# Feed-forward blocks of 768, 768 and 576 tokens instead of 576, 768 and 768, with one product and one addition moved

## The chip, the core and the metric

The kernel runs on one core of a Trainium2 chip. The metric is the device time of one execution in microseconds (us), the median of several runs. The engines are named as in the profile: PE (TensorE, matrix products), PEld (its weight loads), DVE (VectorE), ACT (ScalarE), POOL (GpSimd) and SP (SyncE, which issues most transfers here).

## What is computed

One layer of a streaming encoder over 2048 prompt tokens and 64 sample tokens. The first half (normalisation, the combined input projection, causal convolution, chunk-band attention) is not touched by the change. The second half is, for every token:

```python
merged = sigmoid(g_conv) * conv_out + sigmoid(g_attn) * attn_out
x = x + gt1 * (merged @ w_o)
h2 = rms_norm(x, norm2_g) * (1 + sc2) + sh2
gate, up = split(h2 @ w_ffn_in, 2)            # (1024, 2 * 2816)
x = x + gt2 * ((silu(gate) * up) @ w_ffn_out)  # (2816, 1024)
```

`gt1`, `sc2`, `sh2`, `gt2` come from a conditioning vector of their own for the prompt and for the sample, so the 64 sample tokens need other rows of them.

## The kernel before, in words

**Precision.** Every operand of a product is kept as a high part and a low part (`split`: ACT makes the high part, another engine subtracts it from the source). `mm3` issues three matmuls for each product: high by high, high by low, low by high.

**Blocks.** The second half goes through the tokens in the blocks of `CBLOCKS` (line 36). The sample's 64 tokens are stored ahead of the prompt and lie in the first block, of 576. `token_tiles` cuts a block into tiles of 128 tokens (and one of 64), `tile_chunks` cuts it into two chunks for the merge. For 576 tokens the chunks have 320 and 256 tokens, for 768 they have 384 and 384.

**One block.** For each chunk `merge` multiplies with `w_conv_out` and `w_attn_out` and applies the sigmoid gates, `wo` multiplies with `w_o`, and `residual`, a generator per tile, adds `x`, normalises, transposes and makes the operands `b11 b21 b22 t1 t2 t3 t4` of the next step. Then ten products for the first five gates (`first`, `second`) need `b11` and `b21` alone, which cover the last tiles of `residual`. After them the 22 gates run in pairs (`up`).

**Seven-product scheme, gate and up.** The tokens of a block are taken in two halves and the 1024 inner rows in two halves, so that gate and up column of one `f` are a 2 by 2 by 2 block product with seven products in place of eight: weights `a11 a12 a22` and the sums `s1` to `s4`, each of 128x512. From gate 5 (`EARLY`) on all seven run in this loop, in the order of `up_operands` (line 536): `s2 s3 s1 a12 a22`, `a11` of the next gate, `s4`. Each is 12 matmuls over 288 or 384 columns. Two successive operands make one slab.

**Down product.** In blocks 1 and 2 (`s` true) the pairs of gates 4 to 19 (`PAIRS`) use another seven-product scheme for `w_ffn_out`: `down_pair` with `B11 B21 B22` and the sums `T1` to `T4`, in four groups (`DN`), which `at` places between the products of the next pair at the slabs of `dn_at` (line 544: 0, 1, 3, 4). In block 0 all of it is plain (`down`): eight products' worth for every pair, with no sums. `down` also closes every block with the last gates: it adds the accumulated rows, multiplies by `gt2`, adds the row `x1` (lines 1982 to 1984, all on DVE) and stores the result.

**Weights.** `Weights` loads raw weights, makes the sums on POOL, splits them, and keeps at most five slabs split ahead. The high part is made on ACT, the low part on POOL, or on DVE when the planner's count of POOL's work is more than 4 us ahead of PE's (`BEHIND`, line 456). Sums of gate and up are made once, in block 0, and stored (`sum_d`); in later blocks they are loaded and split again. Weights of kind `fo` and `dn` that are used in more than one block are stored split and then only loaded.

**Order.** `Stream` counts the cost of what has been emitted for each engine; `at(t, f)` runs `f` when PE's count reaches `t`. The order of every engine's queue is thus fixed when the program is built.

Of the kernel before, what the change touches and what calls it, by code (L numbers as in the profile page):

```python
# [35 lines left out]
CBLOCKS = [(0, 576), (576, 1344), (1344, 2112)]  # L36
# [43 lines left out]
def tile_chunks(lo, hi):  # L80

    tiles = token_tiles(lo, hi)
    t, n = tiles[(len(tiles) + 1) // 2 - 1]
    return [(lo, t + n), (t + n, hi)]
# [168 lines left out]
class Weights:  # L253
# [5 lines left out]
    def __init__(self, engines, pool, dram, stream, keys, source, staging, held, kept):  # L259
# [6 lines left out]
        times, raws = {}, {}  # L266
# [119 lines left out]
    def load_on(self, kind):  # L386
        while self.due[kind] and self.free_tag(kind):
            self.load(kind)
# [166 lines left out]
def weight_order():  # L555
# [10 lines left out]
    for s, (lo, hi) in enumerate(CBLOCKS):  # L566
# [13 lines left out]
        yield from (("fo", f) for f in range(NF - 2 if s else NF - 4, NF))  # L580
# [3 lines left out]
def streaming_layer(ctx: ExitStack, tc: tile.TileContext, I, O):  # L584
# [455 lines left out]
    def gate_columns(c0, c1, ct):  # L1040
        g = [half_piece(ct % 2, "tg") for _ in range(2)]
        for j in range(2):
            nc.sync.dma_start(g[j][:, : c1 - c0], g_d[j, ct, :, c0:c1])
        return g

    def load_mixed(c0, c1, i):

        src = [[quarter("cin", i) for _ in range(2)] for _ in range(2)]
        for j, a in enumerate((c_d, o_d)):
            for l in range(2):  # L1050
                nc.sync.dma_start(src[l][j][:, :, : c1 - c0].bitcast(F32), a[l, :, :, c0:c1].rearrange("c p t -> p c t"))
# [546 lines left out]
    def residual(pp, t, n, gt1, a, half, hs, free, last):  # L1598


        which = int(t < SMP)
        x_t = [wk.tile([P, 512], F32, tag="ws", name="x_t", bufs=4) for _ in range(2)]
        for j in range(2):
            nc.sync.dma_start(x_t[j][:n], rows(x_p, x_s, t, n)[:, 512 * j : 512 * j + 512])
# [83 lines left out]
    for s, (lo, hi) in enumerate(CBLOCKS):  # L1688
        tiles = token_tiles(lo, hi)
        half = (hi - lo) // 2  # L1690
        gt1, groups, hs = {}, [], None
        chunks = tile_chunks(lo, hi)
        for i, (c0, c1) in enumerate(chunks):
# [8 lines left out]
            if not groups:  # L1702
                for which in {int(t < SMP) for t, _ in tiles}:
# [39 lines left out]
        hid = [wk.tile([P, 2, 2, CW] if not s else [P, 4, 2, CW // 2], F32R, tag="m0", name="hid"), None]  # L1743
# [40 lines left out]
        def rows_of(f, t, n):  # L1784

            if s:
# [5 lines left out]
        def hidden(f, i, ps):  # L1792
            if s:
# [98 lines left out]
        def up(f, ops, at):  # L1892
# [39 lines left out]
            if f % 2 == 0:  # L1932
# [3 lines left out]
            two = s and f - f % 2 in PAIRS  # L1936
# [15 lines left out]
        def down(fs, ws):  # L1952

            last = fs[-1] == NF - 1
            for i, (t, n) in enumerate(tiles):
# [3 lines left out]
                gt = gt2[int(t < SMP)] if last else None  # L1959
# [12 lines left out]
                for j, ps in enumerate(pss):  # L1972
# [7 lines left out]
                    else:  # L1980
                        if not final:
                            dve.tensor_tensor(ps[:n], ps[:n], dst, ALU.add)
                        dve.tensor_tensor(ps[:n], ps[:n], gt[:n, f], ALU.mult)
                        dve.tensor_tensor(dst, ps[:n], dst if final else x1[j], ALU.add)
                        stream.at(
                            stream.when("dve") + OUT_LAG,
                            lambda t=t, n=n, f=f, dst=dst: nc.sync.dma_start(rows(y_p, y_s, t, n)[:, f], dst),
# [27 lines left out]
        if not s:  # L2015
            W.open("fo", "wfo")
        turns.drain()
# [3 lines left out]
        for f in range(0, NF, 2):  # L2021
            ops = Operands(f)
            if s and f == PAIRS[0]:
                hid[1] = wk.tile([P, 4, 2, CW // 2], F32R, tag="m1", name="hid")
            elif not s and f // 2 % 2 and f >= NF - 4:
                hid[1] = wk.tile([P, 2, 2, CW], F32R, tag="m1", name="hid")

            def at(i, f=f):
                if s and f - 2 in PAIRS:
# [10 lines left out]
        end = NF - 2 if s else NF - 4  # L2040
        ws = [W.get(("fo", f)) for f in range(end, NF)]
        gt2 = {which: gt_row(1, which) for which in {int(t < SMP) for t, _ in tiles}}
# [39 lines left out]
```

## Time and profile before

| | us |
|---|---|
| median of 3 runs | 3047.6 |
| lowest, highest run | 3043.95, 3049.64 |
| profiled execution | 3048.72 |
| its span, first to last instruction | 3046.9 |

The first half of the layer ends at about 1229 us of the span. Block 0 (576 tokens) then runs to about 1785 us, block 1 (768) to about 2409 us and block 2 (768) to the end. Its mean granted TensorE clock is 0.987 of full speed.

In the views below, a row of grouped instructions reads: line, engine, operation, names, form, count, busy time in us, mean ns of one, and the engine's idle time before them with what ended it. A row of a stretch gives its length, then each engine's busy time (with its number of instructions), the granted clock, the busy share of the DMA engines and GB/s. All products come from helpers at one line (L104 is the line of the recorder), so the rows are told apart by tile names: `ps` are the products of gate and up (with `b` or `t` operands) and of the merge (`cin`), `pw` those with `w_o`, `pd` those of the down product; `whi` and `wlo` are the two parts of a weight slab, `wst`, `wup`, `wfo` raw weights, `ws` the weight sums.

### The profile page before, as it was taken

How to read it: one execution, taken by the hardware profiler on the slowest of the kernel's cores; microseconds unless marked ns; L12 is line 12 of the kernel's file. 1: busy time of each engine (PE TensorE's matmuls, PEld its weight loads, DVE VectorE, ACT ScalarE, POOL GpSimd, SP SyncE). 2: the span in 40 equal slices, each digit the busy share in tenths (PEclk: the TensorE clock that was granted, in tenths of full speed). 3: DMA queues.
4: the chain of work that ended last, by engine and by line, in shares of the span. 5: the costliest groups of instructions: out<-in, count | busy, mean ns of one | idle time of the engine just before them, and what ended most of it. 6: DMA issues, size and time to landing. Idle time of an engine off the chain costs nothing. (4 is left out here: it accounts for less than half of the span.)

```text
span 3046.9 us, 44878 instructions
## 1 busy us (share of the span) xinstructions
PE 2936.2 (96%) x16259; PEld 2609.2 (86%) x16259; DVE 2043.0 (67%) x3826; ACT 1254.4 (41%) x2260; POOL 989.7 (32%) x617
## 2 busy tenths in 40 slices
PE   7989898999999999989999999999999999999998
PEld 4789777888878788878998989999999898999997
DVE  4797687877977895467666755655666756366567
ACT  2324432453245257364444424534444244333331
POOL 0200210101011102355677433247767341333331
PEclk9999998999999999999999999999999999999999
DMA  9789788887987788886444686445556965355554
GB/s 336 262 276 309 224 293 267 270 263 265 306 277 247 250 267 274 259 278 218 144 149 142 227 292 202 159 166 190 181 196 202 344 213 189 119 167 174 166 162 174
DMA packets 487084, 693.07 MB, mean 227 GB/s; under 512 B 38485, under 2 KB 316873, under 8 KB 486862
## 3 DMA queue, kind: packets, MB, share of 16 engines
q1 hardware_dynamic: 474581, 672.82, 67.2%
q10 hardware_dynamic: 12280, 17.39, 1.6%
q8 instruction: 128, 2.10, 0.3%
q14 instruction: 95, 0.77, 0.1%
HBM read 505.89 MB, written 184.19 MB: 226 GB/s over the span
## 5 line engine op out<-in xcount | busy, mean ns | idle before, releaser
L104 POOL TENSOR_TENSOR wlo<-wst,whi 128x1024 fp32r<-128x1024 f32 (+1 forms) x180 | 402.6, 2243 | 499.5 <-ACT whi L104 427.6
L104 PE MATMUL ps<-t,whi 128*128 128x384 f32 (+1 forms) x2112 | 505.8, 323 | 10.5 <-DVE t L104 4.8
L104 PE MATMUL pd<-whi,hid 128*128 128x512 f32 (+1 forms) x1400 | 450.3, 391 | 3.4 <-DVE acc L104 3.4
L104 ACT ACTIVATE whi<-wst 128x1024 fp32r<-128x1024 f32 (+1 forms) x269 | 262.0, 978 | 360.5 <-PE ps L104 120.1
L104 PE MATMUL ps<-b,whi 128*128 128x384 f32 (+1 forms) x1584 | 381.1, 326 | 11.4 <-DVE pw L104 4.0
L104 PEld LDWEIGHTS ps<-t,whi 128*128 128x128 f32 x2112 | 370.6, 189 | 18.6 <-ACT u L104 5.5
L104 DVE SCALAR_TENSOR_TENSOR y<-u,wd,y 128x512 f32<-128x512 f32 (+1 forms) x480 | 368.3, 771 | 6.5
L104 PE MATMUL ps<-hh,whi 128*128 128x512 f32 (+2 forms) x992 | 363.6, 367 | 0.0
L104 PE MATMUL ps<-hl,whi 128*128 128x512 f32 (+2 forms) x992 | 346.6, 349 | 0.0
L104 PE MATMUL ps<-hh,wlo 128*128 128x512 f32 (+2 forms) x992 | 346.0, 349 | 0.0
L104 DVE TENSOR_TENSOR acc<-acc,pd 128x512 f32<-128x512 f32 (+1 forms) x440 | 290.5, 684 | 80.4 <-PE pd L104 76.8
L104 PE MATMUL ps<-t,wlo 128*128 128x384 f32 (+1 forms) x1056 | 340.8, 323 | 0.0
L104 PEld LDWEIGHTS pd<-whi,hid 128*128 128x128 f32 (+1 forms) x1400 | 258.1, 184 | 64.7 <-DVE acc L104 6.9
L104 PEld LDWEIGHTS ps<-b,whi 128*128 128x128 f32 x1584 | 278.1, 189 | 14.7 <-DVE pw L104 4.3
L104 PE MATMUL pd<-wlo,hid 128*128 128x512 f32 (+1 forms) x700 | 273.7, 391 | 0.0
L104 PE MATMUL ps<-b,wlo 128*128 128x384 f32 (+1 forms) x792 | 257.1, 325 | 0.0
L104 POOL TENSOR_TENSOR r<-t,mhalf 128x8 f32<-128x8 f32 (+3 forms) x68 | 84.5, 1244 | 390.9 <-DVE t L104 368.0
L104 PEld LDWEIGHTS ps<-hh,wlo 128*128 128x128 f32 x992 | 187.9, 189 | 22.4
L104 POOL TENSOR_TENSOR wlo<-wup,whi 128x1024 fp32r<-128x1024 f32 (+1 forms) x64 | 138.3, 2162 | 208.8 <-ACT whi L104 176.5
L104 PEld LDWEIGHTS ps<-hh,whi 128*128 128x128 f32 x992 | 188.8, 190 | 18.7 <-issue 2.1
L104 PEld LDWEIGHTS ps<-hl,whi 128*128 128x128 f32 x992 | 188.8, 190 | 15.4 <-issue 1.7
L104 PEld LDWEIGHTS ps<-t,wlo 128*128 128x128 f32 x1056 | 199.3, 189 | 0.6
(217 smaller groups left out, 5725.5 us busy)
## 6 DMA issues: line engine op xcount, KB each, us to landing
whi<-w_din_h SPq DMA_DIRECT2D x72, 512.0 KB, 5.9
wlo<-w_din_l SPq DMA_DIRECT2D x72, 512.0 KB, 7.1
wst<-sum_d SPq DMA_DIRECT2D x131, 256.0 KB, 3.0
wmod<-in_w_ada SPq DMA_DIRECT2D x48, 512.0 KB, 8.5
sum_d<-ws SPq DMA_DIRECT2D x88, 256.0 KB, 2.4
wst<-in_w_ffn_in SPq DMA_DIRECT2D x85, 256.0 KB, 3.4
wst<-in_w_ffn_in SPq DMA_DIRECT2D x37, 512.0 KB, 5.4
wst<-in_w_in SPq DMA_DIRECT2D x36, 512.0 KB, 7.1
```

Source lines behind the costliest of these rows:

```text
L104: return f(*args, **kw)
```

## The change

The blocks become (0, 768), (768, 1536) and (1536, 2112). Tokens are renumbered inside the second half: the sample stands at 1536 (`SAT`), at the head of the last block; `stored_at` and `segments` translate to the places where the first half left its results. A range that spans the sample's end needs two transfers. The down product's seven-product scheme is used in blocks 0 and 1 (`SEVEN = 2`), the plain form in block 2. For odd gates from 5 on, `a12` is issued ahead of `s1`; the fourth group of `down_pair` keeps its place behind `s1`, now at slab 5. In the closing `down`, the addition of `x1` goes to GpSimd (`gps`) except in the last two tiles of the last block. Raw `fo` rows of the last block are not loaded before that block's products begin (`limit`), and there only into the two `wfo` buffers.

```diff
-CBLOCKS = [(0, 576), (576, 1344), (1344, 2112)]
+CBLOCKS = [(0, 768), (768, 1536), (1536, 2112)]
+SAT = 1536
+SEVEN = 2
+def block_tiles(lo, hi):
+    head = [(SAT, SMP)] if lo == SAT else []
+    return head + [(u, P) for u in range(lo + SMP * len(head), hi, P)]
+def stored_at(u):
+    return u if u >= SAT + SMP else u - SAT if u >= SAT else u + SMP
+def segments(c0, c1):
+    cuts = [c0] + [c for c in (SAT, SAT + SMP) if c0 < c < c1] + [c1]
+    return [(a - c0, stored_at(a), b - a) for a, b in zip(cuts, cuts[1:])]
...
+            if key[0] == "ca" and n == 2 * SEVEN + 1:
+                self.limit = min(self.limit, len(self.items))
...
-        if kind == "fo" and (self.items[self.due["fo"][0]][0] == "fr" or any(self.items[i][0] == "fi" for i in self.due[""])):
+        if kind == "fo" and (self.limit == 1 << 30 or self.items[self.due["fo"][0]][0] == "fr" or any(self.items[i][0] == "fi" for i in self.due[""])):
             tags = tags[:1]
...
         while self.due[kind] and self.free_tag(kind):
+            if kind == "fo" and self.due[kind][0] >= self.limit:
+                break
...
-    ops = (["s2", "s3", "s1"] if f else ["s3", "s2", "s1"]) + ["a12"] * (f >= EARLY) + ["a22"] + ["a11"] * (EARLY <= f + 1 < NF) + ["s4"]
+    ops = (["s2", "s3"] if f else ["s3", "s2"]) + ["a12"] * (f >= EARLY and f % 2) + ["s1"] + ["a12"] * (f >= EARLY and f % 2 == 0) + ["a22"] + ["a11"] * (EARLY <= f + 1 < NF) + ["s4"]
...
-    return (0, 1, 3, 6 if f == PAIRS[-1] else 4)
+    return (0, 1, 3, 6 if f == PAIRS[-1] else 5)
...
-                if s and f - 2 in PAIRS:
+                if s < SEVEN and f - 2 in PAIRS:
...
         for j in range(2):
-            nc.sync.dma_start(g[j][:, : c1 - c0], g_d[j, ct, :, c0:c1])
+            for o, t, n in segments(c0, c1):
+                nc.sync.dma_start(g[j][:, o : o + n], g_d[j, ct, :, t : t + n])
...
+            def factor():
+                if f >= EARLY:
+                    x = bank("gp")
+                    step(x, "a12", "b21", True, True)
+                    plus(x, x, s1)
+                    silu(c1, x)
+
             if f % 2 == 0:
                 at(0)
+            else:
+                factor()
             step(y, "s1", "t1", False, False)
             plus(v, y, v)
             if f % 2:
-                at(4)
-            if f >= EARLY:
-                x = bank("gp")
-                step(x, "a12", "b21", True, True)
-                plus(x, x, s1)
-                silu(c1, x)
-            if f % 2 == 0:
+                at(5)
+            else:
+                factor()
                 at(1)
...
+                        name = "dve" if hi == T and i >= len(tiles) - 2 else "pool"
                         if not final:
                             dve.tensor_tensor(ps[:n], ps[:n], dst, ALU.add)
-                        dve.tensor_tensor(ps[:n], ps[:n], gt[:n, f], ALU.mult)
-                        dve.tensor_tensor(dst, ps[:n], dst if final else x1[j], ALU.add)
+                        if name == "pool":
+                            dve.tensor_tensor(dst, ps[:n], gt[:n, f], ALU.mult)
+                            stream.after("pool", "dve")
+                            gps.tensor_tensor(dst, dst, x1[j], ALU.add)
+                        else:
+                            dve.tensor_tensor(ps[:n], ps[:n], gt[:n, f], ALU.mult)
+                            dve.tensor_tensor(dst, ps[:n], dst if final else x1[j], ALU.add)
...
         if not s:
             W.open("fo", "wfo")
+        elif not seven:
+            W.limit = 1 << 30
+            W.load_on("fo")
```

Elsewhere `s` is replaced by `seven = s < SEVEN`, `t < SMP` by `t == SAT`, `token_tiles` by `block_tiles`, and the row of `x` or `y` that a tile reads or writes by `stored_at(t)`.

More of the change, by code (lines that the diff above doesn't have):

```diff
@@ L579, in weight_order @@
                     yield from (("fo", f - 2), ("fo", f - 1))
-        yield from (("fo", f) for f in range(NF - 2 if s else NF - 4, NF))
+        yield from (("fo", f) for f in range(NF - 2 if s < SEVEN else NF - 4, NF))
 @with_exitstack
@@ L1688, in streaming_layer @@
     for s, (lo, hi) in enumerate(CBLOCKS):
-        tiles = token_tiles(lo, hi)
+        tiles = block_tiles(lo, hi)
         half = (hi - lo) // 2
+        seven = s < SEVEN
         gt1, groups, hs = {}, [], None
@@ L1702, in streaming_layer @@
             if not groups:
-                for which in {int(t < SMP) for t, _ in tiles}:
+                for which in {int(t == SAT) for t, _ in tiles}:
                     gt1[which] = gt_row(0, which)
@@ L1741, in streaming_layer @@
                 turns.add(gens[i])
-        hid = [wk.tile([P, 2, 2, CW] if not s else [P, 4, 2, CW // 2], F32R, tag="m0", name="hid"), None]
+        hid = [wk.tile([P, 4, 2, CW // 2] if seven else [P, 2, 2, CW], F32R, tag="m0", name="hid"), None]
         early = wk.tile([P, 2 * EARLY - 2, CW // 2], F32, tag="m1", name="early")
@@ L1784, in rows_of @@
         def rows_of(f, t, n):
-            if s:
+            if seven:
                 i, c = divmod(t - lo, half)
@@ L1792, in hidden @@
         def hidden(f, i, ps):
-            if s:
+            if seven:
                 hi, lo = (whole(f, i)[:, j] for j in range(2))
@@ L1935, in up @@
             plus(z, z, u2)
-            two = s and f - f % 2 in PAIRS
+            two = seven and f - f % 2 in PAIRS
             dve.tensor_tensor(z, z, c1, ALU.mult)
@@ L1958, in down @@
                 pss = [ps_g.tile([P, 512], F32, tag="gp", name="pd", bufs=4) for _ in range(2)]
-                gt = gt2[int(t < SMP)] if last else None
+                gt = gt2[int(t == SAT)] if last else None
                 final = last and hi == T and i == len(tiles) - 1
@@ L2039, in streaming_layer @@
         drain()
-        end = NF - 2 if s else NF - 4
+        end = NF - 2 if seven else NF - 4
         ws = [W.get(("fo", f)) for f in range(end, NF)]
-        gt2 = {which: gt_row(1, which) for which in {int(t < SMP) for t, _ in tiles}}
+        gt2 = {which: gt_row(1, which) for which in {int(t == SAT) for t, _ in tiles}}
         x1s = [quarter("x1", 1, F32, (P, 3, 512)) for _ in range(4)]
```

23 lines of the change are left out of this document (13 added, 10 removed).

## The prediction

> **What bounds the kernel now.** I read the page's head first, then stretches of the second half that I cut at the stages of the three blocks.
>
> ```profile
> span 3046.9 us, 44878 instructions
> PE 2936.2 (96%) x16259; PEld 2609.2 (86%) x16259; DVE 2043.0 (67%) x3826; ACT 1254.4 (41%) x2260; POOL 989.7 (32%) x617
> ```
>
> ```profile
> core 0: us, PE busy (x) PEld busy (x) DVE busy (x) ACT busy (x) POOL busy (x), PEclk, DMA share, GB/s
> 1229.00:1340.00 111.00, 106.72 (x622) 94.19 (x623) 59.15 (x118) 51.53 (x83) 44.34 (x21) 0.97 0.82 262
> 1340.00:1425.00 85.00, 72.13 (x443) 66.13 (x443) 56.01 (x99) 47.31 (x91) 48.39 (x36) 0.94 0.77 266
> 1425.00:1720.00 295.00, 291.10 (x1845) 265.17 (x1845) 194.56 (x293) 119.21 (x242) 200.56 (x135) 1.00 0.46 150
> 1785.00:1895.00 110.00, 107.43 (x543) 97.24 (x542) 54.25 (x91) 47.17 (x69) 44.16 (x21) 0.98 0.67 221
> 1895.00:1945.00 50.00, 47.41 (x254) 44.31 (x253) 40.97 (x69) 29.93 (x55) 12.28 (x9) 0.97 0.48 170
> 1945.00:2390.00 445.00, 445.00 (x2341) 417.54 (x2340) 257.17 (x442) 193.04 (x320) 267.74 (x152) 1.00 0.58 192
> 2390.00:2530.00 140.00, 137.79 (x703) 124.38 (x702) 80.17 (x139) 52.49 (x75) 48.00 (x22) 1.00 0.76 256
> 2530.00:2580.00 50.00, 47.37 (x254) 44.45 (x253) 40.53 (x69) 29.92 (x55) 7.04 (x5) 0.97 0.49 172
> 2580.00:3015.00 435.00, 435.00 (x2292) 408.71 (x2291) 249.94 (x431) 157.04 (x258) 153.97 (x65) 1.00 0.50 162
> ```
>
> The first column is the length, the next PE's busy time, so their difference is PE's idle time. In the long stretches of blocks 1 and 2 (1945 to 2390, 2580 to 3015) it is nil: the second half is bound by PE, and there is nothing to win there but matmuls, of which the change removes none. What can move is the idle time at the seams: 4.3 us in block 0's merge (1229 to 1340), 12.9 at its opening (1340 to 1425), 3.9 in its pairs (1425 to 1720), 2.6 in block 1's merge, 2.6 at each of the openings of blocks 1 and 2, and 2.2 where block 1 closes. A wait also costs clock: block 1's opening has a clock of 0.97 over 50 us, that is another 1.5 us behind 2.6 us of idling, block 0's opening 0.94 over 85 us, another 5.1, its merge 0.97 over 111 us, another 3.3. The loss of the openings is thus 18.0, 4.1 and 4.1 us, of block 0's merge 7.6, of block 1's 2.6 + 2.2 (0.98 over 110 us) = 4.8. Then the list of PE's waits in the second half:
>
> ```profile
> PE ps L104 <- DVE t L104: 7.9, 4, 2.4
> PE ps L104 <- DVE pw L104: 4.0, 1, 4.0
> PE ps L104 <- ACT u L104: 3.9, 7, 0.6
> PE ps L104 <- DVE early L104: 3.6, 1, 3.6
> PE pd L104 <- DVE acc L104: 3.4, 6, 0.6
> PE ps L104 <- DVE v L104: 2.8, 2, 1.9
> PE pw L104 <- POOL wlo L104: 2.1, 1, 2.1
> ```
>
> Not one of them is for a weight slab in the pairs: the preparation of weights keeps up everywhere, even in block 0, where it is heaviest.
>
> [...]
>
> **The work is the same.** Two blocks of 768 with seven products and one of 576 with the plain form stand in both kernels, with equal tiles, so the matmuls are equal in number and shape. The sum has only changes of waits.
>
> **1. Openings.** They belong to the block's shape and to what else its engines do. In block 0 the first wait comes from the first splits of the gate weights:
>
> ```profile
> 1348.32 5.01 POOL L104 TENSOR_TENSOR wlo<-wst,whi 128x512 fp32r<-128x512 f32 x4
> 1353.88 1.15 ACT L104 ACTIVATE xn<-x,r 128x1024 f32<-128x1024 f32 x1 [3.81 <-POOL r L104]
> ```
>
> Four low parts hold GpSimd for 5.0 us, the row's inverse root `r` stands behind them, ACT waits 3.8 us, and PE's wait of 3.6 for `early` follows. In the last block these weights come split from memory, so the 576 form there loses this wait, and the waits for `v` (2.8), which I take to stand behind first splits of `fo` on DVE, since `fo` 0 to 3 are only loaded then. What is left is 18.0 - 3.6 - 2.8 - 1.7 (a third of its clock loss) = 9.9. Block 0 in the 768 form: 4.1 as in block 1, plus that ACT wait of 3.8 and 1.7 of clock = 9.6. Block 1: 4.1. Sum 23.6 for 26.2: -2.6. Best, all three like block 1: 12.3, -13.9. Worst, blocks 0 and 2 both like the present block 0: 40.1, +13.9. I stay near the middle, since each half of block 0's loss has a row of its own.
>
> **2. Merges.** The second chunk of 256 tokens waits for gate columns:
>
> ```profile
> 1307.81 0.39 PE L104 MATMUL ps<-cin,whi 128*128 128x256 f32 x1 [2.27 <-DVE t L104]
> ```
>
> Chunks of 384 (blocks 1 and 2) have no such wait. Block 0 gains these 2.3 us and 1.7 of clock; the last block now has the 256 chunk, and twenty more transfers (two for one in the first chunk: sixteen of gates, four of mixed columns) on SP. I give half of it back: -2. Ends -4 and +4.
>
> **3. Handover from block 0 to block 1.** Its 2.1 us wait for `wlo` (4.8 with the clock and what is left of idling) arises where the plain closing with four gates meets the first `w_o` slab; the handover from block 1 to 2, with the form that both will now have, shows only the closing's waits. Half of it: -2.4; ends -4.8 and +3.
>
> **4. Odd gates' `a12`.** It removes and adds nothing, it changes the order.
>
> ```profile
> 1490.74 0.54 PE L104 MATMUL ps<-t,whi 128*128 128x288 f32 x2 [0.56 <-ACT u L104]
> 1527.37 0.53 PE L104 MATMUL ps<-t,whi 128*128 128x288 f32 x2 [0.55 <-ACT u L104]
> ```
>
> Once in a pair (36.6 us) PE waits 0.56 us for ACT's copy of `y` before `s1` accumulates on it; with `a12` between there are twelve more matmuls, well over the wait. All seven waits go: -3.9. In 768 blocks a group of `down_pair` stands there already and no wait shows: 0. Ends -3.9 and 0 (if ACT is late by more).
>
> **5. Closing additions.** Each tile of a 768 block's closing takes DVE three pairs of additions and products:
>
> ```profile
> 3025.68 1.29 DVE L104 TENSOR_TENSOR pd<-pd,acc 128x512 f32<-128x512 f32 x2
> 3028.07 1.27 DVE L104 TENSOR_TENSOR acc<-pd,x 128x512 f32<-128x512 f32 x2
> ```
>
> The third pair is the one that moves; from one tile's start to the end of its third pair are 3.7 us, and PE's 3.4 us for `acc` in six waits (three in each closing) say that it runs out of banks by some 0.6 us a tile. Without the third pair DVE is faster than PE: -3.4. GpSimd gets 12 additions a block, at 1.31 us (below) 15.7 us, in a stretch where it is one third busy (48.0 of 140 us); behind them in its queue stand splits of the next block's merge weights. If those come late like the 2.1 us wait above, with 1.7 of clock, at two handovers: +7.6. Ends -4 and +7.6.
>
> **6. Block 0's pairs.** Here the change adds load: the down sums and splits move from block 1, where they stood alone, to the block that also makes all gate sums.
>
> ```profile
> L104 POOL TENSOR_TENSOR wlo<-wst,whi 128x1024 fp32r<-128x1024 f32 x10 | 24.1, 2411 | 7.0 <-ACT whi L104 7.0
> L104 POOL TENSOR_TENSOR wlo<-ws,whi 128x512 fp32r<-128x512 f32 x8 | 10.3, 1304 | 2.9 <-ACT whi L104 2.9
> L104 POOL TENSOR_TENSOR wlo<-wup,whi 128x1024 fp32r<-128x1024 f32 x4 | 9.6, 2406 | 2.9 <-DMA wfo<-in_w_ffn_out 1.8 <-ACT whi L104 1.2
> L104 POOL TENSOR_TENSOR wlo<-wfo,whi 128x512 fp32r<-128x512 f32 x6 | 7.9, 1315 | 2.9 <-ACT whi L104 2.9
> L104 POOL TENSOR_TENSOR ws<-wfo 128x512 f32<-128x512 f32 x4 | 5.3, 1317 | 10.2 <-DMA wfo<-in_w_ffn_out 10.2
> L104 POOL TENSOR_TENSOR ws<-wfo,ws 128x512 f32<-128x512 f32 x4 | 5.2, 1310 | 0.3
> ...
> L104 DVE TENSOR_TENSOR acc<-acc,pd 128x512 f32<-128x512 f32 x42 | 27.4, 683 | 2.8 <-PE pd L104 2.4
> ```
>
> Two pairs in 88 us (42 additions of `pd`, 21 to a pair): 62.4 us of GpSimd, 31.2 a pair. Block 0's eight gate sums come on top:
>
> ```profile
> L104 POOL TENSOR_TENSOR ws<-wst 128x512 f32<-128x512 f32 x5 | 7.6, 1512 | 3.6 <-DMA wst<-in_w_ffn_in 3.6
> ...
> L104 DVE TENSOR_TENSOR wlo<-ws,whi 128x512 fp32r<-128x512 f32 x10 | 12.4, 1241 | 1.5 <-ACT whi L104 0.9
> L104 DVE TENSOR_TENSOR wlo<-wfo,whi 128x1024 fp32r<-128x1024 f32 x2 | 2.5, 1225 | 1.6 <-ACT whi L104 1.6
> ```
>
> At 1.51 us they take 12.1: 43.3 of 44 us, 98%. But here DVE made at least 14 of the 36 half slabs of two pairs (the 1024 rows count twice). The same share, some 9 of the 21 of a pair, at 1.24 us costs DVE 11 us beside its 25.4 (257.17 of 445 us): 36 of 44, and leaves GpSimd 32. So it fits, as in block 0 now, whose own demand was as near its PE time. What it costs is delay: DVE's 21 additions, 0.683 us each, must follow PE group by group, and a split of 1.24 us among them holds a bank. They fill 14.3 of the 44 us, so 3 of the 9 splits meet them; at half a split each that is 1.9 us a pair, 15 in eight pairs. The nearest row is against it: no wait for `acc` in block 0's pairs at this share. I take +6, nearer to that row. Ends 0 and +42 (rival B).
>
> [...]
>
> **Sum.** -2.6 - 2 - 2.4 - 3.9 - 3.4 + 6 = -8.3. The profiled execution took 3048.7 us (its span and 1.8 around it): 3040.4. The median of the runs is 1.1 lower: 3039.3. I say 3039.
>
> **Rivals.**
> A. The seams shrink more: no first splits at the 576 opening and a longer cover at the 768 one, terms 1 to 3 near their ends (-10, -3, -3.5) and 6 at +2: -21.8, 3026. For it: 10 products over 384 columns cover more than over 288. Against: block 1's opening, with the 384 form and no sums, still waits.
> B. The slower side: weight preparation decides in block 0. GpSimd works in order; in block 1 it stood 10.2 + 1.8 us in 88 waiting for raw `wfo` rows, 6.0 a pair. 43.3 + 6.0 = 49.3 against 44: 5.3 us a pair, 42 in eight, less the lead of slabs split ahead (five, some 4 us each: 20) = 22. It decides once DVE takes fewer than 4 of 21 splits (5.3 / 1.3), or so many that DVE is full (18.6 / 1.24 = 15). Between 22 and 42, at 32 in place of 6: -8.3 + 26 = +17.7, 3065.
> C. Nothing is left: both the 576 and the 768 opening keep block 0's present loss but for one wait, term 1 at +6: sum +0.3, 3048.
> D. The change does not do what it says: the GpSimd additions trade the wait for `acc` for a wait for `wlo`, term 5 at +7.6 with 3 at +3: sum +8.1, 3056.
>
> **Numbers.** Forecast 0.40, A 0.19, B 0.21, C 0.13, D 0.07. The measurement tells 0.2%, about 6 us, from no change: faster means below 3041.5, slower above 3053.7. Of the forecast's cases 0.34 lie below and 0.06 between; A is faster; C counts as 0.12 same and 0.01 slower; B is 0.20 slower and 0.01 same, D 0.06 and 0.01. Faster 0.53, same 0.20, slower 0.27. The forecast's own range is 3030 to 3047; to hold 8 in 10 I go down through most of A to 3016 and up through the middle of B to 3067.
>
> **What would show it.** Step 4: no row of PE waiting for ACT `u` in the plain pairs. Step 5: no PE wait for DVE `acc` at the closings, GpSimd rows `acc<-acc,x` of about 1.3 us. Step 1: idle of some 5 us at the first opening, 2.6 at the second, 6 to 8 at the third. Step 6: in block 0's pairs a PE idle time of a few us, DVE at 80% and GpSimd near 75%; rival B shows as PE waits for `whi`, `wlo` or `acc` in a row of pairs longer than 44 us. The forecast is wrong if those pairs lose more than 20 us, or if the openings together lose under 15 or over 35.

## The result and the profile after

| | before | after |
|---|---|---|
| median of 4 runs, us | 3048.62 | 3068.32 |
| lowest, highest run | 3043.95, 3050.93 | 3064.48, 3072.30 |
| profiled execution | 3048.72 | 3071.78 |
| its span | 3046.9 | 3070.0 |
| mean granted TensorE clock | 0.987 | 0.985 |

The ratio of the times is 1.0065, with a 95% interval of 1.0050 to 1.0079: the changed kernel is slower by 15 to 24 us. The forecast of 3039 had the wrong sign, and the range (3016 to 3067) ended 1.3 us below the median. In the changed kernel the recorder's line is L123 instead of L104. The head of its page first:

```profile
span 3070.0 us, 44879 instructions
PE 2946.5 (96%) x16259; PEld 2611.7 (85%) x16259; DVE 2021.8 (66%) x3828; ACT 1254.1 (41%) x2260; POOL 986.2 (32%) x615
```

The matmuls are the same 16259, as the prediction had it; PE's 10.3 us of added busy time are matmuls that took longer or overlapped less, of which more below. The stretches of the second half, cut at the stages of its three blocks (columns as before: length, busy time of each engine, granted clock, DMA share, GB/s):

```profile
1229.00:1330.00 101.00, 99.15 (x532) 92.75 (x532) 53.54 (x96) 45.20 (x68) 40.85 (x19) 1.00 0.82 280
1330.00:1440.00 110.00, 102.13 (x506) 92.96 (x505) 69.67 (x116) 55.27 (x102) 48.63 (x36) 0.95 0.67 225
1500.00:1880.00 380.00, 359.97 (x1842) 327.55 (x1841) 281.65 (x460) 162.61 (x323) 216.96 (x161) 1.00 0.57 194
1900.00:1950.00 50.00, 43.59 (x223) 42.15 (x222) 26.41 (x45) 14.41 (x18) 23.30 (x14) 0.90 0.97 329
2060.00:2110.00 50.00, 47.59 (x257) 45.84 (x256) 36.44 (x58) 23.87 (x41) 7.77 (x3) 0.97 0.49 161
2110.00:2535.00 425.00, 425.00 (x2231) 398.50 (x2230) 245.98 (x424) 153.59 (x251) 160.72 (x69) 1.00 0.52 169
2550.00:2600.00 50.00, 44.05 (x243) 38.50 (x242) 19.90 (x34) 16.39 (x20) 19.18 (x9) 0.93 0.94 295
2600.00:2680.00 80.00, 77.86 (x488) 70.29 (x487) 54.33 (x111) 48.71 (x90) 23.71 (x14) 0.98 0.74 247
2740.00:3060.00 320.00, 319.69 (x2020) 291.83 (x2019) 138.32 (x258) 121.40 (x197) 185.32 (x81) 1.00 0.43 136
```

Two stages stand out. Block 0's pairs (1500 to 1880) leave PE idle for 20.0 us at a mean clock of 1.00, where block 1's, with the same matmuls but ready sums (2110 to 2535), leave it idle for none. And each handover has a stretch in which the DMA engines are full (0.97, 0.94) and PE loses 6 us and clock (1900 to 1950: 6.4 us at 0.90; 2550 to 2600: 6.0 us at 0.93). Then the list of PE's waits in the second half:

```profile
PE ps L123 <- DVE t L123: 21.2, 7, 6.4
PE ps L123 <- DVE acc L123: 7.9, 4, 2.9
PE pd L123 <- DVE acc L123: 6.4, 9, 1.6
PE pd L123 <- DVE s L123: 4.3, 4, 3.4
```

The seven waits for ACT's `u` are gone, and waits for `acc` and `s` (which free banks) are new in the pairs. `t` has grown from 7.9 to 21.2 us. That name stands for two tiles: in the merges its waits grew from 3.1 to 14.5 us (6.4, 6.0 and 2.1), in the openings from 4.8 to 6.6.

To add up the losses I took, in both traces, the interval from each matmul's start to the next and subtracted the median interval of its shape. What is left over is the time lost in a stage, waits, slow clock and longer intervals between matmuls together (the same count is made for the experiments below):

| stage | before | after | difference |
|---|---|---|---|
| block 0: merge | 7.6 | 3.1 | -4.5 |
| block 0: opening | 18.8 | 15.3 | -3.5 |
| block 0: pairs | 6.1 | 33.6 | +27.5 |
| handover 0 to 1, merge | 5.4 | 10.7 | +5.3 |
| block 1: opening | 5.0 | 4.4 | -0.6 |
| block 1: pairs | 2.7 | 3.0 | +0.3 |
| handover 1 to 2, merge | 4.0 | 12.1 | +8.1 |
| block 2: opening | 5.3 | 3.9 | -1.4 |
| block 2: pairs, closing | 5.4 | 0.9 | -4.5 |
| from the last matmul's start to the end | 8.3 | 4.7 | -3.6 |

The sum, +23.1, is the difference of the two profiled executions (3071.78 - 3048.72 = 23.1).

**Where block 0's pairs lose.** Of the 33.6 us there, 20.0 show as idle time of PE. The rest is inside its busy time, in longer intervals from one matmul's start to the next. Where the pair quoted below leaves PE idle for 2.90 us, the interval is 3.24 us (1757.94 to 1761.18), for 0.17 at the median of these matmuls, and the next weight load's own wait is 3.22. The list of PEld's waits between 1500 and 1880 us holds both kinds:

```profile
PEld ps L123 <- DVE acc L123: 9.2, 4, 3.2
PEld pd L123 <- DVE acc L123: 8.9, 17, 0.7
PEld pd L123 <- DVE s L123: 7.1, 7, 3.9
PEld pd L123 <- ACT whi L123: 5.4, 3, 1.9
PEld ps L123 <- ACT s L123: 1.0, 1, 1.0
```

Together 31.6 us, all behind DVE or ACT, although DVE is busy for 74% of that stretch (281.65 of 380 us) and GpSimd for 57%. Nobody is short of time; something makes them stand. One pair's timeline shows what (start, duration, instruction, and in brackets the engine's idle time before it and what ended it; the order is that of the steps):

```profile
1748.69 1.62 POOL L123 TENSOR_TENSOR ws<-wup 128x512 f32<-128x512 f32 x1
1756.92 1.29 POOL L123 TENSOR_TENSOR ws<-ws,wst 128x512 f32<-128x512 f32 x1 [6.61 <-DMA sum_d<-ws]
...
1758.24 0.63 ACT L123 ACTIVATE whi<-ws 128x512 fp32r<-128x512 f32 x1 [4.79 <-POOL ws L123]
...
1758.91 0.69 DVE L123 TENSOR_TENSOR wlo<-ws,whi 128x512 fp32r<-128x512 f32 x1 [3.73 <-ACT whi L123]
...
1760.45 0.68 DVE L123 TENSOR_TENSOR acc<-acc,pd 128x512 f32<-128x512 f32 x1
...
1761.18 0.62 PE L123 MATMUL ps<-b,whi 128*128 128x384 f32 x2 [2.90 <-DVE acc L123]
```

GpSimd stands 6.6 us until a store of an earlier sum to `sum_d` has landed. ACT, in order, stands 4.8 us for that sum; DVE, in order, 3.7 us for ACT's high part; the addition `acc<-acc,pd` that frees a bank of PE is behind it in DVE's queue; PE stands 2.9 us. In block 0's pairs GpSimd meets this once a pair:

```profile
POOL ws L123 <- DMA sum_d<-ws: 45.8, 8, 6.6
```

The same follows in all eight pairs. In seven of them PE's longest wait of the pair ends 4.3 us after the late sum begins, in the first 6.2 us after it. Another pair of rows:

```profile
1615.62 1.29 POOL L123 TENSOR_TENSOR ws<-ws,wst 128x512 f32<-128x512 f32 x1 [5.88 <-DMA sum_d<-ws]
...
1619.88 0.47 PE L123 MATMUL pd<-whi,hid 128*128 128x512 f32 x1 [1.49 <-DVE acc L123]
```

These eight waits of PE sum to 15.9 of its 20.0 us of idle time.

All sums, the gates' `s1` to `s4` and the down product's `T1` to `T4`, are made in the same four buffers `ws`. A gate sum leaves its buffer only when its store has landed. `T1` and `T2` are made early in a pair, and are held until they are split for the third group. So with the down sums in block 0 a gate sum finds two of four buffers taken and waits for a store. In the kernel before, no block made both kinds in its pairs.

**Where the handovers lose.** The closing's waits for `acc` are gone and the merge begins sooner, but its gate columns do not. SyncE's queue and the two engines that wait for it, block 0 to 1:

```profile
1908.08 1.80 SPq L399 DMA_DIRECT2D wst<-in_w_attn_out  x1
...
1912.73 8.28 SPq L2026 DMA_DIRECT2D out<-acc  x12
...
1922.61 1.07 SPq L1067 DMA_DIRECT2D tg<-g_d  x2
...
1927.10 0.56 DVE L123 SCALAR_TENSOR_TENSOR t<-tg,ps 128x384 f32<-128x384 f32 x1 [10.56 <-DMA tg<-g_d]
...
1927.80 0.98 PE L123 MATMUL ps<-cin,whi 128*128 128x384 f32 x2 [6.41 <-DVE t L123]
```

The twelve stores of the closing take SyncE 8.3 us to issue (0.69 each, while the DMA engines are full), the third pair of gate columns is issued only behind them, and PE waits 6.4 us for it. The clock falls as well. Cut finer, the same stretch shows where:

```profile
1923.70:1927.80 4.10, 0.00 (x0) 0.03 (x1) 0.70 (x2) 1.06 (x1) 0.47 (x1) 0.50 1.01 319
1927.80:1933.80 6.00, 6.00 (x19) 6.00 (x20) 4.11 (x8) 2.04 (x3) 4.27 (x2) 0.50 1.02 375
```

The clock is at half for some 10 us, but 4 of them lie inside the wait. The matmuls lose about half of the other 6, some 3 us (0.32 us from one start to the next, where it is 0.18 at a clock of 1.00), and not the 5.0 that the mean of 0.90 over 50 us suggests. That fits the table: 10.7 us for the whole handover.

### The profile page after: what moved, and what is told of

Read it like the earlier page. It is cut to its first block, busy times and chain, and to the rows that moved or that the text cites. A ratio compares the mean times of both kernels' runs of the same rounds, so it can differ in the third digit from the quotient of the medians.

```text
span 3070.0 us, 44879 instructions
## 1 busy us (share of the span) xinstructions
PE 2946.5 (96%) x16259; PEld 2611.7 (85%) x16259; DVE 2021.8 (66%) x3828; ACT 1254.1 (41%) x2260; POOL 986.2 (32%) x615
## 5 line engine op out<-in xcount | busy, mean ns | idle before, releaser
L123 POOL TENSOR_TENSOR wlo<-wst,whi 128x1024 fp32r<-128x1024 f32 (+1 forms) x170 | 377.8, 2228 | 515.0 <-ACT whi L123 440.2
L123 PE MATMUL ps<-t,whi 128*128 128x384 f32 (+1 forms) x2112 | 507.2, 324 | 9.9 <-DVE t L123 6.6
L123 PE MATMUL pd<-whi,hid 128*128 128x512 f32 (+1 forms) x1400 | 456.4, 393 | 11.5 <-DVE acc L123 6.4
L123 ACT ACTIVATE whi<-wst 128x1024 fp32r<-128x1024 f32 (+1 forms) x269 | 261.0, 975 | 406.9 <-PE ps L123 120.6
L123 PEld LDWEIGHTS ps<-t,whi 128*128 128x128 f32 x2112 | 371.6, 189 | 20.4 <-DVE t L123 7.7
L123 PE MATMUL ps<-b,whi 128*128 128x384 f32 (+1 forms) x1584 | 379.3, 325 | 10.1 <-DVE acc L123 7.9
L123 DVE SCALAR_TENSOR_TENSOR y<-u,wd,y 128x512 f32<-128x512 f32 (+1 forms) x480 | 368.5, 771 | 6.5
L123 PE MATMUL ps<-hh,whi 128*128 128x512 f32 (+2 forms) x992 | 363.4, 366 | 0.0
L123 DVE TENSOR_TENSOR acc<-acc,pd 128x512 f32<-128x512 f32 (+1 forms) x440 | 290.1, 683 | 89.2 <-PE pd L123 86.3
L123 PE MATMUL ps<-hl,whi 128*128 128x512 f32 (+2 forms) x992 | 346.3, 349 | 0.0
L123 PE MATMUL ps<-hh,wlo 128*128 128x512 f32 (+2 forms) x992 | 345.7, 349 | 0.0
L123 PE MATMUL ps<-t,wlo 128*128 128x384 f32 (+1 forms) x1056 | 341.5, 323 | 0.0
L123 PEld LDWEIGHTS pd<-whi,hid 128*128 128x128 f32 (+1 forms) x1400 | 258.5, 185 | 79.2 <-DVE acc L123 8.9
L123 PEld LDWEIGHTS ps<-b,whi 128*128 128x128 f32 x1584 | 276.3, 188 | 13.0 <-DVE acc L123 9.2
L123 PE MATMUL pd<-wlo,hid 128*128 128x512 f32 (+1 forms) x700 | 274.3, 392 | 0.0
L123 PE MATMUL ps<-b,wlo 128*128 128x384 f32 (+1 forms) x792 | 256.1, 324 | 0.0
L123 POOL TENSOR_TENSOR r<-t,mhalf 128x8 f32<-128x8 f32 (+3 forms) x68 | 84.8, 1249 | 404.3 <-DVE t L123 374.6
L123 POOL TENSOR_TENSOR wlo<-wup,whi 128x1024 fp32r<-128x1024 f32 (+1 forms) x61 | 137.7, 2258 | 220.6 <-ACT whi L123 202.5
L123 PEld LDWEIGHTS ps<-hh,wlo 128*128 128x128 f32 x992 | 187.6, 189 | 22.4
L123 PEld LDWEIGHTS ps<-hh,whi 128*128 128x128 f32 x992 | 188.5, 190 | 18.7 <-issue 2.1
L123 PE MATMUL ps<-cin,whi 128*128 128x384 f32 (+2 forms) x768 | 188.2, 331 | 15.9 <-DVE t L123 14.5
L123 PEld LDWEIGHTS ps<-hl,whi 128*128 128x128 f32 x992 | 188.5, 190 | 15.4 <-issue 1.7
```

The lines of the kernel that those rows point to most:

```text
L123: return f(*args, **kw)
```

## The experiments

The first theory is that of the buffers. Its first rival is load: GpSimd, DVE and ACT have too much to do in block 0. Times are medians; ratios, with their 95% intervals, are against the kernel before on the same chip (3046.9 for four runs: the early group, the odd gates' order alone, the order undone and the additions on DVE; 3047.7 for the rest).

**The third down group one slab earlier.** `T1` and `T2` are then split, and leave their buffers, one slab sooner. All work stays, though not on the same engine, as shown below.

```diff
-    return (0, 1, 3, 6 if f == PAIRS[-1] else 5)
+    return (0, 1, 2, 6 if f == PAIRS[-1] else 5)
...
-            if f % 2:
-                at(3)
...
                 copy(begun[f + 1][1], ny)
+            if f % 2 == 0:
+                at(2)
```

> The changed kernel with one move: the third group of the down pair (T2, T1) comes one slab earlier, behind a11 of the next gate instead of behind s2 of the odd gate, so that both sums leave their two of the four ws buffers before s4, s1 and s2 are made. Theory of the buffers (block 0's pairs lose some 30 us because GpSimd waits up to 6.6 us in each pair for a ws buffer whose store to memory has not landed, ACT waits for that sum, DVE for ACT's high part and PE for DVE's additions): GpSimd's idle time before ws<-ws,wup and ws<-ws,wst by sum_d falls from 46 us in block 0 to under 15, PE's idle time between 1500 and 1880 from about 20 us to under 8, and the time falls by 12 to 25 us, to 3043 to 3056. Rival of the load (DVE has too many splits among its additions): the number of splits on DVE stays, and so does the loss; the time moves by less than 5 us.

Measured: 3042.5 us (0.9982, 0.9972 to 0.9991), 25.9 below the changed kernel. GpSimd's waits for a store and PEld's waits between 1500 and 1880 us:

```profile
POOL ws L123 <- DMA sum_d<-ws: 2.6, 2, 2.2
```

```profile
PEld pd L123 <- DVE acc L123: 4.7, 9, 1.1
PEld pd L123 <- DVE s L123: 3.8, 2, 2.0
PEld pd L123 <- issue: 0.6, 1, 0.6
```

The waits for the store fall from 45.8 to 2.6 us, PEld's from 31.6 to 9.1, and block 0's pairs lose 11.6 us in place of 33.6. To compare the engines over the same work, here are the pairs up to the closing, in the changed kernel and with the early group:

```profile
1456.00:1888.00 432.00, 411.97 (x2116) 376.31 (x2115) 311.45 (x511) 181.70 (x356) 242.05 (x179) 1.00 0.56 192
1454.00:1861.00 407.00, 402.62 (x2104) 374.62 (x2104) 333.49 (x536) 182.51 (x355) 206.21 (x149) 1.00 0.59 201
```

DVE is busy for 22 us more (82% of the stretch, where it was 72%), and the stage is 25 us shorter: the opposite of what load on DVE as the cause would give.

But the run changed a second thing. In these pairs the planner gave DVE 132 of the low parts' half slabs (128x512) in place of 103, and GpSimd 52 in place of 85; GpSimd's busy time falls from 242 to 206 us. So a lighter GpSimd is a rival that this run does not separate. The other runs limit it. With the third group at its old place, and 101 and 135 half slabs on GpSimd (the next experiment, and the order undone), the store waits stay at 42.7 and 42.0 us and the pairs lose 6.0 and 8.3 us more. If that goes on in the other direction, 33 half slabs fewer are worth some 5 to 12 us, an estimate, of the 22. The late group with fewer splits on GpSimd was not run.

**DVE's share of the splits.** With `BEHIND` at 12 us in place of 4, DVE takes fewer of the splits.

```diff
-BEHIND = 4000.0
+BEHIND = 12000.0
```

> The changed kernel with BEHIND at 12 us instead of 4, so that fewer low parts go to DVE. Theory of the buffers: GpSimd's waits for sum_d stay, GpSimd carries more, and block 0's pairs lose as much or more: 0 to 30 us slower than the changed kernel. Rival of the load on DVE: with fewer splits among the additions PE's waits for acc shrink and the time falls by 8 us or more.

Measured: 3067.6 us (1.0066, 1.0049 to 1.0084), the same as the changed kernel. In block 0's pairs (1500 to 1880 us) DVE makes 75 half slabs of low parts in place of 95, and is busy for 264 in place of 282 us. The pairs lose 39.7 us, 6 more than in the changed kernel, and the merges and the last opening win about as much. Splits on DVE are thus not what costs the time.

**Is an earlier third group better anyway?** The kernel before, with the odd gates' new order and with the same move of the group (the diff is the one above; the place of the fourth group is that of the change).

> The kernel before with the odd gates' new order, and with the third down group one slab earlier, in the old blocks. Theory: that group's early place helps only where the down sums T1 and T2 hold two of the four buffers that the gate sums need too; in the old blocks the pairs with down sums (blocks 1 and 2) make no gate sums, so nothing is released: 3040.6 as with the new order alone, within 3 us, and no wait of 3 us of GpSimd for a store of sums in blocks 1 and 2. Rival: the place of the group is better of itself (banks, work on DVE): below 3035.

Measured: 3039.5 us (0.9964, 0.9951 to 0.9977), against 3040.6 (0.9979, 0.9970 to 0.9989) with the order alone, the next experiment: 1.1 us by the medians, 4.6 by the ratios, and the intervals overlap. The move that takes 25.9 us from the changed kernel takes at most a few where the two kinds of sum do not meet.

**The odd gates' order alone**, in the blocks of before.

```diff
-    ops = (["s2", "s3", "s1"] if f else ["s3", "s2", "s1"]) + ["a12"] * (f >= EARLY) + ["a22"] + ["a11"] * (EARLY <= f + 1 < NF) + ["s4"]
+    ops = (["s2", "s3"] if f else ["s3", "s2"]) + ["a12"] * (f >= EARLY and f % 2) + ["s1"] + ["a12"] * (f >= EARLY and f % 2 == 0) + ["a22"] + ["a11"] * (EARLY <= f + 1 < NF) + ["s4"]
...
+            else:
+                factor()
             step(y, "s1", "t1", False, False)
```

> The kernel before with the new order of the odd gates alone. Theory: the seven waits for ACT u go, 3.9 us of idling (some 5 with the refilling of the pipeline), nothing else changes: 3 to 6 us faster than before. Rival: PE waits elsewhere in the same pair and the time stays within 1 us.

Measured: 3040.6 us (0.9979, 0.9970 to 0.9989), 6.3 below the kernel before. Counted as in the table, block 0's pairs lose 0.6 us in place of 6.1. The waits were worth more than their listed 3.9. At each of the seven, 0.85 to 0.86 us pass from the start of the last matmul ahead of the wait to the next one's, and 0.23 from that one's to the one after it, where the median is 0.13: some 0.83 us each, 5.8 in all.

**The order undone in the changed kernel** (the same diff, reversed).

> The changed kernel with the old order of the odd gates (s1 ahead of a12, the fourth group at slab 4). Theory: the plain pairs, now in the last block, get their wait of 0.56 us for ACT u back, seven or eight times, and in block 0 s1 leaves its ws buffer one slab earlier, which shortens GpSimd's waits a little: sum between -6 and +6 us. Rival (the move of a12 itself costs block 0 its stalls, since s1 holds a buffer for one more slab): block 0's pairs lose less than 10 us and the time falls by 15 to 25 us.

Measured: 3077.7 us (1.0099, 1.0084 to 1.0114), 9.4 above the changed kernel, more than expected. The waits for `u` did not come back in the last block; the loss is in block 0's pairs:

```profile
PE pd L123 <- DVE acc L123: 16.3, 11, 2.8
PE pd L123 <- DVE s L123: 9.9, 8, 3.7
```

26.2 us, for 18.6 in the changed kernel (7.9 + 6.4 + 4.3 in the list above). GpSimd's waits for the stores are no longer than before (42.0 us), so the old order does not lose by them. GpSimd makes 135 half slabs of low parts here in place of 85, and PEld's waits for ACT's high parts have grown from 5.4 to 16.0 us. Which of the two, the order or the splits, costs the time is open.

**The closing additions back on DVE**, in the changed kernel.

```diff
-                        name = "dve" if hi == T and i >= len(tiles) - 2 else "pool"
+                        name = "dve"
```

> The changed kernel with the closing addition of x1 back on DVE. Theory of the queue at the handover (PE waits some 6 us in the third gate column of the merge, because the columns' transfers stand in SP's queue behind the block's twelve stores and the loads before them, on DMA engines that are full): the closing waits for acc come back (about 0.55 us in each of three or four places a block), the waits for t shrink by about the same amount, and the time stays within 4 us of the changed kernel. Rival (GpSimd's additions make the stores or the splits late): the waits for t of 6.4 and 6.0 us fall under 2 us each and the time falls by 8 to 14 us.

Measured: 3062.2 us (1.0047, 1.0032 to 1.0062), 6.1 below the changed kernel; the interval overlaps that of the changed kernel (1.0050 to 1.0079). The time lies between the two expectations, and the waits for `t` fell as the rival said, to 0.5 and 1.2 us. The handover from block 0 to 1 (1880 to 1960 us) now has these waits:

```profile
PE pd L123 <- DVE acc L123: 1.7, 3, 0.6
PE ps L123 <- DVE acc L123: 0.6, 1, 0.6
PE ps L123 <- DVE t L123: 0.5, 1, 0.5
```

Five waits of at most 0.6 us, 2.8 in all, stand in the place of one of 6.4, behind which the clock was 0.50 for another 6.0 us. The third pair of gate columns is issued 12.5 us after the merge's first matmul (1923.70 and 1911.24) in place of 18.3 (1922.61 and 1904.27). The closing is slower by 3.5 us, and two weight loads that stood ahead of that pair, 1.4 us of issuing, now stand behind it. Counted from the closing's first matmul to the merge's last, the two handovers lose 5.1 and 7.6 us in place of 9.8 and 11.6.

**The stores on ACT's queue**, so that the gate columns pass them.

```diff
-                            lambda t=t, n=n, f=f, dst=dst: nc.sync.dma_start(rows(y_p, y_s, stored_at(t), n)[:, f], dst),
+                            lambda t=t, n=n, f=f, dst=dst: nc.scalar.dma_start(rows(y_p, y_s, stored_at(t), n)[:, f], dst),
```

> The changed kernel with the stores of the block's result issued by ACT instead of SP. Theory of the queue at the handover (the third gate column's transfers stand behind twelve stores in SP's queue, 8.3 us of issuing): those transfers are issued some 8 us earlier, PE's waits for t of 6.4 and 6.0 us in the merges fall under 1.5 us each, with the half clock behind them, and the time falls by 8 to 15 us. Rival (the DMA engines are full there and the columns land no earlier, whoever issues): the waits stay above 4 us and the time within 4 us.

Measured: 3063.0 us (1.0054, 1.0037 to 1.0070), 5.3 below the changed kernel by the medians and 3.4 by the ratios, whose intervals overlap: no gain that is clear of noise. The waits are what the rival said, above 4 us: 4.2 and 4.7 us remain, now for DVE's `m`, a later step of the same chain, which needs ACT's copy `m`. ACT's timeline shows why that is late:

```profile
1912.65 1.06 ACT L123 ACTIVATE whi<-wst 128x1024 fp32r<-128x1024 f32 x1 [7.98 <-DMA wst<-in_w_attn_out]
1913.61 0.47 ACT L123 ACTIVATE m<-ps 128x384 fp32r<-128x384 f32 x1
```

The copy stands behind a high part, and ACT waits 8.0 us for that one's raw weights (`wst`) to land. The DMA engines are full here too (share 1.07 between 1900 and 1925 us). So SyncE's queue is not the whole of it: the merge's loads themselves land late.

**Two of them together.** The early group with the stores on ACT, then the early group with the additions on DVE.

> The changed kernel with the third group one slab earlier and the result's stores on ACT. If both causes are right and independent, the gains add up: 26 us of the first and 8 to 15 of the second, 3027 to 3035. If the second is not right: about 3042.

Measured: 3043.8 us (0.9982, 0.9972 to 0.9992), which is the second of the two cases.

> The changed kernel with the third group one slab earlier and the closing addition on DVE. The addition's place was worth 6 us in the changed kernel; if that comes from the handover alone it is worth the same here: 3034 to 3039. If it came from block 0's pairs by way of GpSimd's load, it is gone: 3040 to 3045.

Measured: 3041.5 us (0.9980, 0.9971 to 0.9990). Neither differs measurably from the early group alone (3042.5, 0.9982). With the additions on DVE no wait of over 2 us is left at the handover from block 0 to 1, yet the time is only 1 us lower: the 6 us that the additions on GpSimd cost in the changed kernel are not a fixed price. Block 0's pairs up to the closing lose the same with and without them (10.8 and 10.7 us), so it is not GpSimd's load there. The handover from block 0 to 1 already loses less with the early group alone, 6.6 us in place of 9.8, and the additions on DVE make it 7.7; the one from 1 to 2 falls from 10.5 to 7.1.

**The order of the blocks by itself**: the early group and the additions on DVE, with the old order of the odd gates.

> The changed kernel's blocks alone, with the third down group one slab earlier so that the buffers' wait is mostly gone; the odd gates' old order, the closing additions on DVE. Against 3041.5 of the kernel that differs from it in the odd gates' order alone. Theory: the order's 9 us in the changed kernel came mostly from the buffers' waits in block 0, so here it is worth only its wait for u in the plain pairs, 4 us, and those come back (seven waits for ACT u of some 0.55 us in the last block): 3044 to 3048, that is, the new order of the blocks by itself gains nothing. Rival: the odd gates' order is worth 9 us in any case: 3050 or more, the blocks' order costs.

Measured: 3045.3 us (0.9996, 0.9986 to 1.0007): no difference from the kernel before. It lies in the theory's range, but not for the reason that I gave. The waits for `u` did not come back in the last block; all of PE's waits there (2740 to 3030 us) are one for a weight:

```profile
PE pd L123 <- DMA wlo<-w_dfo_l: 0.5, 1, 0.5
```

So what made `u` late belongs to block 0, and the new blocks take these waits away without the odd gates' new order. The 3.8 us between this run and the one before it lie at the edge of their intervals, and are left open. They are not in block 0's pairs, which lose 5.8 us up to the closing here and 10.8 in the run before: with the early group the old order costs nothing there.

More than four buffers `ws` would test the first theory most directly. That was not tried. So it is shown that the place of the third group decides, that it is worth little where the two kinds of sum do not meet, that the waits for the stores go with it, and that each of them is followed by PE's longest wait of its pair. How much of the 22 us the lighter GpSimd gave is open, and that a fifth buffer alone would do the same is argued.

## Why the prediction was wrong

**Step 6, block 0's pairs, is the one that failed.** It said that what the added load costs is delay, a DVE split meeting an addition, and took +6 of 0 to +42, leaning on the row that showed no wait for `acc`. The runs: +27.5. PE does wait for DVE's additions, but DVE itself stands behind a sum that GpSimd could not begin: 45.8 us of waiting for stores in eight pairs. By its own sign (pairs that lose more than 20 us) the forecast was wrong. The share of DVE was foreseen well enough (80%, measured 74%) and that of GpSimd was put too high (near 75%, measured 57%), but shares were the wrong thing to ask for. I counted instructions and busy time, and not buffers: which tile each sum lies in, how long it stays there, and what must land before the next can be made. The early group, which shortens that holding time, gives 25.9 us back, 22 of them in these pairs. "So it fits" was true of the engines and false of the four buffers.

**Rival B** had the place (weight preparation decides in block 0) and the size (22 to 42, at 32, and 3065 for the whole). Its mechanism was another, GpSimd short of time and raw `wfo` rows late, and the trace is against it: GpSimd is idle for 43% of the stretch, and it waits for stores of sums, not for `wfo`. Neither of its conditions held, since DVE took 103 of 188 half slabs, some 11 of 21, between its 4 and its 15. That a lighter GpSimd helps by some us is not excluded, as said above.

**Steps 3 and 5, the handovers and the closing.** They were to give -2.4 and -3.4. The handovers and merges of blocks 1 and 2 lost 13.4 us more instead (about 4 of them are step 2's). The wait for `wlo` of step 3 went, as it said. Step 5's sign at its own place was right: no wait for `acc` at the closings, and GpSimd's additions take 1.27 us each:

```profile
1900.40 2.54 POOL L123 TENSOR_TENSOR acc<-acc,x 128x512 f32<-128x512 f32 x2 [0.17 <-DVE acc L123]
```

What failed is that the time won there was counted as won: the next stage's gate columns came no sooner. Rival D foresaw that the additions trade one wait for another, but put it on `wlo` behind GpSimd; it was on the transfers.

**Step 2, the merges.** Block 0 gained 4.5 us, near the 4.0 of the step. The last block was to give half of it back; the second half of its merge (2600 to 2680, with its chunk of 256 tokens) lost 4.0 of the 12.1 us, so nearly all of the gain was given back.

**Step 1, the openings.** -2.6 was forecast, and -5.5 came (-3.5 - 0.6 - 1.4). The first is still the most costly one (7.9 us of idling between 1330 and 1440), at 15.3 us where the step had 9.6; the third cost 3.9, where it had 9.9: without first splits the 576 form opens as the 768 form does (4.4 in block 1). Two terms missed by some 6 us each, in opposite directions. That the sum came out near is luck.

**Step 4, `a12`.** The waits for `u` went, as forecast, and alone the new order is worth 6.3 us, above the 3.9. In the changed kernel they would have gone without it, as the two runs with the old order show. The step's other half, that it is worth nothing in 768 blocks, failed (9.4 us); by which way is open.

**Not foreseen in this form:** 3.6 us at the very end and 4.5 in the last block. Of the 4.5, 2.7 are the closing's waits for `acc`, which step 5 meant to win by GpSimd; the runs with the additions on DVE have lost at most 0.7 there as well. Before, DVE closed the last tiles back to back, 5.1 us behind PE's last matmul; now it waits for PE before each step. The end of DVE's work before and after:

```profile
3038.61 0.39 PE L104 MATMUL pd<-whi,hid 128*128 128x512 f32 x1
...
3042.43 1.27 DVE L104 TENSOR_TENSOR acc<-pd,acc 128x512 f32<-128x512 f32 x2
```

```profile
3065.26 0.39 PE L123 MATMUL pd<-whi,hid 128*128 128x512 f32 x1
...
3065.69 0.70 DVE L123 TENSOR_TENSOR pd<-pd,gt 128x512 f32<-128x512 f32 x1 [1.29 <-PE pd L123]
3066.42 0.69 DVE L123 TENSOR_TENSOR acc<-pd,acc 128x512 f32<-128x512 f32 x1
```

It was 3043.70 - 3038.61 = 5.1 us and is 3067.11 - 3065.26 = 1.9. The runs with the additions on DVE end in the same way, so both belong to the plain closing of the last block, not to GpSimd's additions.

In sum, the steps other than 6 and the handovers gave -18 us (-4.5 - 3.5 - 0.6 + 0.3 - 1.4 - 4.5 - 3.6), more than all that was forecast; step 6 took 27.5 and the handovers 13.4.

## What to carry to other kernels

When a change brings two producers into one stage, count the buffers they share as well as the engines' time: for each buffer who fills it, until when it is held, and whether a transfer must land before it is free. With engines that work in order, one late buffer passes through all of them to the matmuls while none of DVE, ACT and GpSimd is over three quarters busy, as in block 0's pairs here (GpSimd waits 6.6 us in the pair shown, ACT 4.8, DVE 3.7 and PE 2.9; the busy shares of the stretch are 57%, 43% and 74% for the first three). And time won at the end of a stage is won only if what the next stage loads is asked for sooner as well; here PE waited 6.4 and 6.0 us for it.

## What the runs showed of the hardware

**The clock fell after some short waits and not after others.** Between 2060 and 2110 us PE idles for 2.4 us, in one wait that ends at 2076.18 us, and the granted clock over the 50 us is 0.97. Cut finer, it is 1.00 up to 2077.2, then at half, and 1.00 again from 2080.7:

```profile
2077.30:2080.60 3.30, 3.30 (x12) 3.20 (x11) 3.30 (x6) 1.01 (x2) 0.00 (x0) 0.50 0.66 187
```

Behind the longer wait of 2.90 us that ends at 1761.18 us, quoted above, it stays at 1.00:

```profile
1758.00:1761.18 3.18, 0.28 (x2) 0.00 (x1) 2.27 (x5) 2.60 (x6) 1.49 (x2) 1.00 0.23 86
1761.18:1764.00 2.82, 2.82 (x15) 2.73 (x16) 2.82 (x6) 0.90 (x2) 2.72 (x3) 1.00 0.25 92
1764.00:1770.00 6.00, 5.63 (x26) 4.30 (x25) 6.00 (x10) 1.40 (x4) 4.34 (x3) 1.00 0.91 323
```

So the length of a wait alone does not tell in these traces whether the clock falls, and the prediction's "a wait also costs clock" held for some of them. With the early group and the additions on DVE, PE idles for 2.0 us between 1880 and 1950 us, in waits of at most 1.9 us, at a clock of 1.00.

**DVE splits of one shape took 0.69 us with GpSimd standing, and up to 1.77 beside its work.** The one at 1758.91 above, with GpSimd standing, took 0.69. The one below ran beside GpSimd's sum of 1748.69 (1.62 us, for about 1.29 elsewhere) and took 1.31, with the same shape:

```profile
1749.55 1.31 DVE L123 TENSOR_TENSOR wlo<-wst,whi 128x512 fp32r<-128x512 f32 x1
```

In the second half of this kernel 62 such splits ran with GpSimd standing, at 0.68 to 0.69 us. The 46 that GpSimd's work covered for the most part took 0.68 to 1.77, 1.16 on the mean, and the 11 that it covered for a lesser part 0.68 to 0.91. The prediction's 1.24 for a split was the mean of ten that took 0.69 to 1.99.

**Some transfers took longer to issue where the DMA engines were full.** SyncE took 1.80 us to issue the load `wst<-in_w_attn_out` at 1908.08 us, quoted above, where the DMA share is 1.08 (1900 to 1913). The loads of that tensor over the whole kernel (count, and shortest, median and longest time in ns):

```profile
L399 SPq DMA_DIRECT2D wst<-in_w_attn_out x37: 373/502/1986, 293.9 to 2621.0; - x37
```

The median is 0.50. The three that took over 1 us (1.99, 1.80 and 1.40) lie where the DMA share is 1.10 and 1.12 (1903 to 1913, 2543 to 2550 us), and the other 34 took at most 0.86. The stores were late twice there, in being issued and in landing: the twelve of 1912.73 us, at a share of 1.07, took 0.67 us each to issue (median) and 4.2 to 4.7 to land, where the last block's ten, at 0.46 (3040 to 3068 us), took 0.33 and 2.0. Full engines are not the only place of slow issues: two loads of the same tensor into `wup` took 1.72 and 1.42 us at shares of 0.66 and 0.39 (1276 to 1281, 2502 to 2506 us).
